# Output and down projections of a two-layer decoder trunk, with weights moved 512 wide and a residual that keeps tokens on partitions

## The chip, the cores and the metric

The kernel runs on one core of a Trainium2 chip. The metric is the device time of one execution in microseconds (us). One execution was also taken by the hardware profiler; its rows are what this document reads.

## The reference, cut to what matters

256 tokens of width 2048 go through two layers. Each layer normalises, projects to three groups of attention heads (4 differential, 6 latent, 6 forgetting), joins the 16 heads and projects back; then it normalises again and runs a gated MLP of width 5632 with a short convolution over the tokens. A last norm ends the trunk. The lines that the change touches are these:

```python
mix = jnp.concatenate([o_a, o_b, o_c], axis=-1)              # 16 heads x 128
x = x + jnp.einsum('bsm,md->bsd', mix, w_o[l])               # output projection
h = _rmsnorm(x, ffn_norm[l])
x = x + _conv_gated_mlp(h, ffn_w_up[l], ffn_conv_w[l], ffn_conv_b[l], ffn_w_down[l])
...
return _rmsnorm(x, final_norm)
```

`_conv_gated_mlp` ends with the down projection, `silu(g) * a` (256 x 5632) times `w_down` (5632 x 2048). The norm is `x * rsqrt(mean(x*x) + eps) * gain` over the 2048 features.

## The kernel before

All weights lie in memory as one stream of 128x128 blocks, in the order of use. SyncE loads 16 blocks at a time (1 MB, `load`), three such chunks in flight. `convert` splits 8 blocks at a time (a "sub") into a rounded part `hi` (ScalarE, L134) and the rest `lo` (VectorE, L135); four subs of each exist, and `weights` asks for a sub two ahead of the one in use. Activations are kept split in the same way, as one tile of 512 columns: `hi` of the 256 tokens, then `lo`. A product is hi*hi + hi*lo + lo*hi.

Two helpers build most matmuls. `mm_t` (L184 to L188) has the weight block stationary and the activations moving: per block one matmul of 512 columns (weight `hi` against both halves of the activations) and one of 256 (weight `lo` against the first half). Its result has features on partitions and tokens along the free dimension. `mm_v` (L218 to L220) turns the roles round: 128 tokens of an activation tile are stationary and 512 (or 256) columns of weights move; per step there are three matmuls for each of the two token halves, which cover four blocks. Before the change only the value projections use `mm_v`.

The residual `xT` has features on partitions: 16 tiles of 128 features x 256 tokens. The output projection runs in two passes over 16 feature tiles: pass 1 over 10 heads (L717 on), while the last six heads' attention is worked off in the background by `tick()`; pass 2 over the remaining six heads (L725 on). Each tile's result is added to `xT[m]` by two VectorE instructions (L718/719, L726/727, and L763/764 in the down projection). In pass 2 and in the second half of the down projection `norm.add` follows: ScalarE squares the tile (L350), GpSimd sums the squares (L355), ScalarE and VectorE write the next stage's split input `h` (L359, L360). `norm.cols` then sums the squares over partitions with four small matmuls (L324), and `norm.rows` spreads the factors over partitions (L339).

The MLP runs in two halves of 22 tiles; each half ends with a down projection of 16 feature tiles with 22 blocks each. After the last one every tile is scaled by the final gain (L768), the factors are spread, and VectorE multiplies eight tiles (L772), each followed by its store.

The order of instructions on each engine comes from the program order of this code, with small moves by the tile framework; a wait is a semaphore set between engines. Three PSUM banks serve the tiles called `mm`, two the tiles called `s`.

Of the kernel before, what the change touches and what calls it, by code (L numbers as in the profile page):

```python
# [58 lines left out]
def kernel(ctx: ExitStack, tc: tile.TileContext, xin, pos, wstream, cst, par, fin, out):  # L59
# [174 lines left out]
    gfin = const.tile([P, KT], F32, tag="gfin", name="gfin")  # L234
    pint = work.tile([P, T], I32, tag="tmp", name="pint", bufs=15)
    xg = [big.tile([P, 2, T], F32, tag=f"x{k}", name=f"x{k}") for k in range(KT // 2)]
# [140 lines left out]

    def score_mm(parts, bias=None):
# [100 lines left out]
    for l in range(DEPTH):  # L479
# [11 lines left out]
        else:  # L491
            first = mm_t2(hx, {KT // 2: norm.cols})
# [4 lines left out]
        if l == 0:  # L497
# [3 lines left out]
            nc.sync.dma_start(gfin, fin)  # L501
# [220 lines left out]
        norm = Norm(q_[:, Q_FN : Q_FN + KT], D)  # L722
        hx = [big.tile([P, 2 * T], F32R, tag=f"h{k}", name=nm("h")) for k in range(KT)]
        for m in range(KT):
            ps = mm_t([mix[i] for i in range(4, 10)])  # L725
            nc.vector.tensor_tensor(xT[m], xT[m], ps[:, :T], ALU.add)  # L726
            nc.vector.tensor_tensor(xT[m], xT[m], ps[:, T : 2 * T], ALU.add)  # L727
            norm.add(xT[m], m, hx[m])
        rstd = None

        for half in range(2):
            acts = []
            for i in range(HALF):
                ft = half * HALF + i
                ys = []
                for j in range(2):
                    ps = mm_t(hx, {KT // 2: norm.cols} if rstd is None else {})
                    rstd = rstd or norm.rows("rstd")
                    u = total(ps)
# [13 lines left out]
            last = half == 1  # L753
            if last:
                final = l == DEPTH - 1
                if not final:
                    norm = Norm(pr[l + 1][:, Q_AN : Q_AN + KT], D)
                    hx = [big.tile([P, 2 * T], F32R, tag=f"h{k}", name=nm("h")) for k in range(KT)]
                else:
                    norm = Norm(None, D)  # L760
            for m in range(KT):
                ps = mm_t(acts)
                nc.vector.tensor_tensor(xT[m], xT[m], ps[:, :T], ALU.add)  # L763
                nc.vector.tensor_tensor(xT[m], xT[m], ps[:, T : 2 * T], ALU.add)
                if last:
                    norm.add(xT[m], m, None if final else hx[m])
                    if final:
                        nc.scalar.activation(xT[m], xT[m], AF.Copy, scale=gfin[:, m : m + 1])  # L768

    rows = spread((norm.cols(), norm.dg)[1]).rearrange("p (j t) -> p j t", j=1).to_broadcast([P, 2, T])  # L770
    for g in range(KT // 2):
        nc.vector.tensor_tensor(xg[g], xg[g], rows, ALU.mult)  # L772
        (nc.sync, nc.scalar)[g % 2].dma_start(out[g], xg[g])


def _layout(inputs):
# [20 lines left out]
    for l in range(DEPTH):  # L797
# [25 lines left out]
        stat(np.concatenate([wo[10 * P :], wo[: 4 * P]], axis=0))  # L823
        stat(wo[4 * P : 10 * P])
        up, dn = w["ffn_w_up"][l], w["ffn_w_down"][l]
        for half in range(2):
            for i in range(half * HALF, (half + 1) * HALF):
                stat(up[:, i * P : (i + 1) * P])
                stat(up[:, FF + i * P : FF + (i + 1) * P])
            stat(dn[half * HALF * P : (half + 1) * HALF * P])  # L830
# [11 lines left out]
    for l in range(DEPTH):  # L842
# [30 lines left out]
        "x": np.ascontiguousarray(w["x"].reshape(T, KT // 2, 2, P).transpose(1, 3, 2, 0)),  # L873
        "pos": np.ascontiguousarray(np.broadcast_to(w["positions"].reshape(1, T), (P, T))),
# [3 lines left out]
        "fin": np.ascontiguousarray(w["final_norm"].reshape(KT, P).T),  # L878
# [20 lines left out]
```

## Time and profile before

| what | value |
|---|---|
| median of 3 timed runs (2298.13 to 2301.83) | 2298.94 us |
| the profiled execution, its span from first to last instruction | 2297.5 us |
| median of the runs less that span | 1.44 us |
| matmuls | 12956 |
| TensorE busy | 2270.6 us, 99% |
| VectorE busy | 1580.0 us, 69% |
| ScalarE busy | 1234.2 us, 54% |
| mean granted TensorE clock | 0.997 |

The page has no own time for the profiled execution beside its span. A busy time of TensorE counts matmuls that overlap: ends are modelled, so what a matmul costs is read from the distance between two starts, not from its length.

### The profile page before, as it was taken

The numbers are of one execution on the slowest core, as the hardware profiler recorded it, in microseconds if no ns is written. First come the engines' busy times: TensorE is split into PE (matmuls) and PEld (weight loads), VectorE is DVE, ScalarE is ACT, GpSimd is POOL, SyncE is SP. The second block draws the span as 40 slices with busy tenths as digits, with TensorE's granted clock in tenths as the row PEclk, the third lists the DMA queues.
The fourth block names the chain that finished last, engine by engine and source line by source line (L and its number), as shares of the span: only waits on it lengthen the run. The fifth ranks groups of instructions, "written<-read, shape, count | busy, mean of one in ns | idle before, by whom it ended". The sixth has DMA issues, their size and how long they took to land.

```text
span 2297.5 us, 33344 instructions
## 1 busy us (share of the span) xinstructions
PE 2270.6 (99%) x12956; PEld 1965.8 (86%) x12956; DVE 1580.0 (69%) x2512; ACT 1234.2 (54%) x1878; POOL 447.6 (19%) x445
## 2 busy tenths in 40 slices
PE   8999999999999999999999999999999999999997
PEld 7888988888888888888888889888888888888886
DVE  7768768777765577776664777687777556777654
ACT  6456645655543455554454665466555435555543
POOL 5500002222210022221140110032222001222211
PEclk9999999999999999999999999999999999999999
DMA  7544434555555555555555444345555555555553
GB/s 257 186 163 165 149 140 171 183 183 186 188 187 190 184 184 185 185 191 185 189 185 183 152 162 164 129 173 189 188 184 183 186 187 191 188 184 183 185 186 116
DMA packets 60062, 410.59 MB, mean 179 GB/s; under 512 B 6912, under 2 KB 7040, under 8 KB 11136
## 3 DMA queue, kind: packets, MB, share of 16 engines
q1 hardware_dynamic: 59184, 407.40, 49.8%
q8 instruction: 101, 1.65, 0.3%
q10 hardware_dynamic: 720, 1.07, 0.1%
q14 instruction: 57, 0.47, 0.1%
HBM read 406.35 MB, written 2.10 MB: 178 GB/s over the span
## 4 chain that ended last, share of the span: by engine, by line
PE 96%; DVE 3%; issue 1%; ACT 0%; DMA 0%; POOL 0%; DVEq 0%; ACTq 0%
PE mm L184 52%; PE mm L185 26%; PE mm L188 3%; PE mm L218 2%; PE mm L219 2%; PE mm L220 2%; PE s L386 2%; PE mm L187 2%; DVE h L360 1%; PE mm L205 1%; DVE lo L135 1%; PE mm L678 1%; PE mm L679 1%; PE mm L680 1%; PE pv L418 1%
## 5 line engine op out<-in xcount | busy, mean ns | idle before, releaser
L135 DVE TENSOR_TENSOR lo<-raw,hi 128x1024 fp32r<-128x1024 f32 (+1 forms) x775 | 988.7, 1276 | 454.3 <-ACT hi L134 449.7
L184 PE MATMUL mm<-h,hi 128*128 128x512 f32 x3435 | 1225.4, 399 | 0.6 <-DVE x L727 0.6
L134 ACT CAST hi<-raw 128x1024 fp32r<-128x1024 f32 (+1 forms) x775 | 807.4, 1042 | 596.7 <-PE mm L184 444.8
L185 PE MATMUL mm<-h,lo 128*128 128x256 f32 x3435 | 964.1, 281 | 0.0
L184 PEld LDWEIGHTS mm<-h,hi 128*128 128x128 f32 x3435 | 645.5, 188 | 151.6 <-issue 1.7
L185 PEld LDWEIGHTS mm<-h,lo 128*128 128x128 f32 x3435 | 648.5, 189 | 9.8
L184 PE MATMUL mm<-slot,hi 128*128 128x512 f32 x1792 | 640.0, 399 | 3.4 <-DVE x L727 3.4
L185 PE MATMUL mm<-slot,lo 128*128 128x256 f32 x1792 | 503.1, 281 | 0.0
L184 PEld LDWEIGHTS mm<-slot,hi 128*128 128x128 f32 x1792 | 336.7, 188 | 87.0 <-issue 5.1
L185 PEld LDWEIGHTS mm<-slot,lo 128*128 128x128 f32 x1792 | 338.4, 189 | 4.7
L741 POOL TENSOR_TENSOR tmp<-tmp,rstd 128x256 f32<-128x256 f32 x176 | 131.1, 745 | 736.3 <-DVE tmp L229 721.2
L227 ACT COPY tmp<-mm 128x256 f32<-128x256 f32 (+1 forms) x233 | 86.7, 372 | 161.1 <-PE mm L188 159.5
L749 POOL TENSOR_TENSOR tmp<-tmp,tmp 128x256 f32<-128x256 f32 x88 | 120.2, 1366 | 268.6 <-ACT tmp L748 264.9
L355 POOL TENSOR_TENSOR tmp<-tmp,tmp 128x256 f32<-128x256 f32 x64 | 78.5, 1227 | 454.1 <-ACT tmp L350 453.3
L744 ACT ACTIVATE tmp<-tmp,par 128x256 f32<-128x256 f32 x176 | 105.7, 601 | 66.5 <-POOL tmp L741 66.4
L229 DVE TENSOR_TENSOR tmp<-mm,tmp 128x256 f32<-128x256 f32 (+1 forms) x233 | 97.6, 419 | 53.2 <-ACT tmp L227 53.1
L424 DVE TENSOR_TENSOR slot<-tmp,slot 128x256 fp32r<-128x256 f32 x96 | 41.2, 429 | 92.5 <-ACT slot L423 92.5
L423 ACT CAST slot<-tmp 128x256 fp32r<-128x256 f32 x96 | 39.0, 406 | 108.0 <-POOL tmp L749 106.3
L188 PE MATMUL mm<-h,hi 128*128 128x512 f32 x229 | 91.4, 399 | 0.0
L746 DVE SCALAR_TENSOR_TENSOR tmp<-tmp,par,tmp 128x254 f32<-128x254 f32 x176 | 85.0, 483 | 6.2
L745 DVE SCALAR_TENSOR_TENSOR tmp<-tmp,par,tmp 128x255 f32<-128x255 f32 x176 | 83.3, 473 | 1.3 <-ACT tmp L744 1.3
L218 PE MATMUL mm<-hi,h 128*128 128x512 f32 (+1 forms) x192 | 68.3, 356 | 0.0
(183 smaller groups left out, 1815.0 us busy)
## 6 DMA issues: line engine op xcount, KB each, us to landing
raw<-in_w SPq DMA_DIRECT2D x381, 1024.0 KB, 4.8
raw<-in_w SPq DMA_DIRECT2D x12, 256.0 KB, 5.4
x<-in_x SPq DMA_DIRECT2D x8, 256.0 KB, 5.3
out<-x SPq DMA_DIRECT2D x4, 256.0 KB, 2.3
out<-x ACTq DMA_DIRECT2D x4, 256.0 KB, 2.4
raw<-in_w SPq DMA_DIRECT2D x1, 512.0 KB, 3.4
par<-in_par SPq DMA_DIRECT2D x1, 325.0 KB, 6.3
par<-in_par SPq DMA_DIRECT2D x1, 304.0 KB, 5.2
```

The costliest lines, as they stand in the source:

```text
L134: nc.scalar.copy(hi[:, a], src[:, a])
L135: nc.vector.tensor_tensor(lo[:, a], src[:, a], f(hi[:, a]), ALU.subtract)
L184: nc.tensor.matmul(ps, hi, mv, start=(i == 0), stop=False)
L185: nc.tensor.matmul(ps[:, :T], lo, mv[:, :T], start=False, stop=False)
L188: nc.tensor.matmul(ps, hi, mv, start=False, stop=True)
L218: nc.tensor.matmul(ps[t][:, :n], s_hi, hi, start=(i == 0), stop=False)
L227: nc.scalar.copy(t[:rows], ps[:rows, T : 2 * T])
L229: nc.vector.tensor_tensor(u[:rows], ps[:rows, :T], t[:rows], ALU.add)
L741: nc.gpsimd.tensor_tensor(uu, u, rstd, ALU.mult)
L744: nc.scalar.activation(y, uu, AF.Identity, scale=q_[:, w + 2 : w + 3], bias=q_[:, w + 3 : w + 4])
L746: nc.vector.scalar_tensor_tensor(y[:, 2:], uu[:, : T - 2], q_[:, w : w + 1], y[:, 2:], ALU.mult, ALU.add)
L749: nc.gpsimd.tensor_tensor(ys[0], ys[0], ys[1], ALU.mult)
```

## The change

The output projection and the down projection use `mm_v` with 512 columns of weights moving, so their results have tokens on partitions. The residual becomes `xr`, two tiles of 128 tokens x 2048 features; it is loaded by two transfers of 1 MB. The first layer's input still comes in with features on partitions (into slots that are free later). `residual` runs four column groups j of 512 features; after each, two VectorE adds of 512 columns follow. In a stage that feeds a norm, ScalarE squares and sums each piece (`RowNorm.add`), and eight TensorE transposes (`RowNorm.turn`) bring four feature tiles back to features on partitions, hooked in before step 2 of the next column group (the last four tiles: before step 4 of the next projection). The first pair of up-projection tiles is built by `mm_t2`, which interleaves two feature tiles. The final gain is multiplied in by GpSimd (the last group by VectorE), and the output is stored with tokens on partitions.

```diff
-    def mm_v(stat, n, every):
+    def mm_v(stat, n, every, hooks={}):
...
+            if i in hooks:
+                hooks[i]()
...
-            if i % every == every - 1:
+            if every and i % every == every - 1:
                 tick()
...
+    xr = [big.tile([P, D], F32, tag=f"x{t}", name=f"x{t}") for t in range(2)]
+    xg = [slot().rearrange("p (j t) -> p j t", j=2) for k in range(KT // 2)]
...
+    class RowNorm:
...
+        def add(self, j, t):
+            a = slice(j * 512, (j + 1) * 512)
+            nc.scalar.activation(slot(), xr[t][:, a], AF.Square, accum_out=self.sums[:, t, j : j + 1])
+
+        def turn(self, j):
+            for g in range(2):
+                ps = bank("s", 2)
+                ks = [4 * j + 2 * g + i for i in range(2)]
+                for i, k in enumerate(ks):
+                    for t in range(2):
+                        o = i * T + t * P
+                        nc.tensor.transpose(ps[:, o : o + P], xr[t][:, k * P : (k + 1) * P], ident)
+                for i, k in enumerate(ks):
+                    x, hl, gk = ps[:, i * T : (i + 1) * T], self.hl[k], self.gain[:, k : k + 1]
+                    nc.scalar.activation(hl[:, :T], x, AF.Copy, scale=gk)
+                    nc.vector.scalar_tensor_tensor(hl[:, T : 2 * T], x, gk, f(hl[:, :T]), ALU.mult, ALU.subtract)
+
+        def cols(self):
...
+                nc.vector.tensor_reduce(r, self.sums, mybir.AxisListType.X, ALU.add)
+                nc.scalar.activation(r, r, AF.Sqrt, scale=1.0 / D, bias=e_main)
+                nc.vector.reciprocal(r, r)
...
+    def residual(stat, every, after=None):
+        for j in range(4):
+            ps = mm_v(stat, 512, every, {2: (lambda: after(j - 1))} if after and j else {})
+            for t in range(2):
+                a = slice(j * 512, (j + 1) * 512)
+                nc.vector.tensor_tensor(xr[t][:, a], xr[t][:, a], ps[t], ALU.add)
+                if after:
+                    norm.add(j, t)
...
-            first = mm_t2(hx, {KT // 2: norm.cols})
+            first = mm_t2(hx, {4: lambda: norm.turn(3), KT // 2: norm.cols})
...
-            nc.sync.dma_start(gfin, fin)
+            for t in range(2):
+                nc.sync.dma_start(xr[t], xnat[t])
...
-        for m in range(KT):
-            ps = mm_t([mix[i] for i in order])
-            nc.vector.tensor_tensor(xT[m], xT[m], ps[:, :T], ALU.add)
-            nc.vector.tensor_tensor(xT[m], xT[m], ps[:, T : 2 * T], ALU.add)
-            tick()
+        residual([mix[i] for i in order], 2)
...
+        norm = RowNorm(q_[:, Q_FN : Q_FN + KT], hx)
+        residual([mix[i] for i in range(4, 10)], 0, norm.turn)
...
+                    pair = mm_t2(hx, {4: lambda: norm.turn(3), KT // 2: norm.cols})
+                    rstd = norm.rows("rstd")
...
+            if half == 0:
+                residual(acts, 0)
+            elif l < DEPTH - 1:
...
+                residual(acts, 0, norm.turn)
+            else:
+                gf = [slot() for _ in range(4)]
+                for j in range(4):
+                    nc.sync.dma_start(gf[j], fin[:, j * 512 : (j + 1) * 512])
...
+                        e = nc.vector if j == 3 else nc.gpsimd
+                        e.tensor_tensor(xr[t][:, a], xr[t][:, a], gf[j], ALU.mult)
...
+    col = norm.cols()
+    for j in range(4):
+        a = slice(j * 512, (j + 1) * 512)
+        nc.vector.tensor_scalar(xr[0][:, a], xr[0][:, a], col[:, 0:1], None, ALU.mult)
+        nc.sync.dma_start(out[0][:, a], xr[0][:, a])
+        nc.scalar.activation(xr[1][:, a], xr[1][:, a], AF.Copy, scale=col[:, 1:2])
+        nc.scalar.dma_start(out[1][:, a], xr[1][:, a])
```

The weight stream keeps its blocks and its length; within these projections they are laid down row by row of 512 columns.

The order on TensorE in the last down projection. Before, each weight block (`hi`, `lo`) is the stationary operand of two matmuls, named behind the comma, and one activation tile (`slot`) moves:

```order
L184 MATMUL mm_21719<-slot_18524,hi_21663 128x512
L185 MATMUL mm_21719<-slot_18524,lo_21664 128x256
L184 MATMUL mm_21719<-slot_18635,hi_21663 128x512
L185 MATMUL mm_21719<-slot_18635,lo_21664 128x256
L184 MATMUL mm_21719<-slot_18746,hi_21663 128x512
L185 MATMUL mm_21719<-slot_18746,lo_21664 128x256
L184 MATMUL mm_21719<-slot_18857,hi_21663 128x512
L185 MATMUL mm_21719<-slot_18857,lo_21664 128x256
```

After, the `slot` is stationary and 512 columns of `hi` or `lo` move; two accumulators (one for each half of the tokens) take turns:

```order
L220 MATMUL mm_20362<-hi_20486,slot_19540 128x512
L221 MATMUL mm_20362<-lo_20487,slot_19540 128x512
L222 MATMUL mm_20362<-hi_20486,slot_19540 128x512
L220 MATMUL mm_20363<-hi_20486,slot_19540 128x512
L221 MATMUL mm_20363<-lo_20487,slot_19540 128x512
L222 MATMUL mm_20363<-hi_20486,slot_19540 128x512
```

Four blocks stand for eight matmuls in the first piece and for six in the second.

The order on VectorE in pass 2 of layer 0. Before (L726, L727 are the adds, L360 writes the second half of `h`, L135 is the conversion of weights):

```order
L726 TENSOR_TENSOR x_78<-x_78,mm_3747 128x256
L727 TENSOR_TENSOR x_78<-x_78,mm_3747 128x256
L360 SCALAR_TENSOR_TENSOR h_3708<-x_78,par_73,h_3708 128x256
L135 TENSOR_TENSOR lo_3799<-raw_3696,hi_3798 128x1024
L360 SCALAR_TENSOR_TENSOR h_3709<-x_78,par_73,h_3709 128x256
L726 TENSOR_TENSOR x_79<-x_79,mm_3767 128x256
L135 TENSOR_TENSOR lo_3827<-raw_3772,hi_3826 128x1024
L727 TENSOR_TENSOR x_79<-x_79,mm_3767 128x256
L726 TENSOR_TENSOR x_79<-x_79,mm_3793 128x256
L727 TENSOR_TENSOR x_79<-x_79,mm_3793 128x256
L360 SCALAR_TENSOR_TENSOR h_3710<-x_79,par_73,h_3710 128x256
```

After (L426 are the adds, L401 writes `h` from the transposed tiles `s`), from the end of column group 0 to the end of column group 1:

```order
L426 TENSOR_TENSOR x_77<-x_77,mm_3615 128x512
L135 TENSOR_TENSOR lo_3682<-raw_3643,hi_3681 128x1024
L426 TENSOR_TENSOR x_78<-x_78,mm_3616 128x512
L135 TENSOR_TENSOR lo_3718<-raw_3643,hi_3717 128x1024
L401 SCALAR_TENSOR_TENSOR h_3598<-s_3693,par_73,h_3598 128x256
L401 SCALAR_TENSOR_TENSOR h_3600<-s_3702,par_73,h_3600 128x256
L401 SCALAR_TENSOR_TENSOR h_3599<-s_3693,par_73,h_3599 128x256
L401 SCALAR_TENSOR_TENSOR h_3601<-s_3702,par_73,h_3601 128x256
L135 TENSOR_TENSOR lo_3734<-raw_3685,hi_3733 128x1024
L426 TENSOR_TENSOR x_77<-x_77,mm_3673 128x512
L135 TENSOR_TENSOR lo_3760<-raw_3685,hi_3759 128x1024
L426 TENSOR_TENSOR x_78<-x_78,mm_3674 128x512
```

Eight adds of 256 columns per four feature tiles have become two of 512; the four writes of `h` stay, and now wait for TensorE's transposes.

## Rows read from the trace of the kernel before

**Rows 1.** The page: busy time and share of the span; the chain by engine.
```profile
PE 2270.6 (99%) x12956; PEld 1965.8 (86%) x12956; DVE 1580.0 (69%) x2512; ACT 1234.2 (54%) x1878; POOL 447.6 (19%) x445
...
PE 96%; DVE 3%; issue 1%; ACT 0%; DMA 0%; POOL 0%; DVEq 0%; ACTq 0%
```

**Rows 2.** Windows by stage: stretch, length, busy us by engine, granted clock, DMA.
```profile
287.90:362.80 74.90, 74.90 (x413) 61.74 (x412) 50.69 (x124) 32.74 (x57) 0.00 (x0) 1.00 0.42 150
362.80:413.30 50.50, 47.24 (x266) 40.00 (x265) 45.78 (x73) 31.35 (x53) 17.67 (x15) 1.00 0.47 167
...
650.60:775.60 125.00, 124.80 (x706) 107.91 (x705) 67.06 (x79) 47.69 (x48) 2.20 (x2) 1.00 0.52 185
...
1498.60:1548.60 50.00, 47.54 (x266) 40.08 (x265) 45.78 (x72) 31.12 (x53) 17.68 (x15) 1.00 0.47 169
...
1786.00:1910.40 124.40, 124.40 (x706) 107.87 (x705) 67.10 (x78) 47.78 (x48) 2.04 (x2) 1.00 0.52 186
...
2283.60:2297.50 13.90, 1.84 (x9) 1.45 (x8) 6.78 (x14) 2.47 (x4) 0.00 (x0) 0.60 0.40 151
```

**Rows 3.** Timeline of TensorE, first column the start: down projection, its first matmul and the next stage's.
```profile
650.63 0.40 PE L184 MATMUL mm<-slot,hi 128*128 128x512 f32 x1
...
775.59 0.40 PE L184 MATMUL mm<-h,hi 128*128 128x512 f32 x1
```

**Rows 4.** Timeline of TensorE: a value projection, 96 matmuls of 512 columns, then 256.
```profile
88.07 0.40 PE L218 MATMUL mm<-hi,h 128*128 128x512 f32 x1
...
109.84 0.28 PE L218 MATMUL mm<-hi,h 128*128 128x256 f32 x1
...
110.20 0.29 PE L218 MATMUL mm<-hi,h 128*128 128x256 f32 x1
```

**Rows 5.** Timeline of TensorE: transposes of one head and the matmuls behind them.
```profile
176.20 0.27 PE L409 MATMUL pt<-cs,tmp 128*128 128x128 f32 x1
176.31 0.27 PE L410 MATMUL pt<-cs,tmp 128*128 128x128 f32 x1
...
176.45 0.48 PE L218 MATMUL mm<-hi,h 128*128 128x512 f32 x1
176.76 0.40 PE L219 MATMUL mm<-lo,h 128*128 128x512 f32 x1
```

**Rows 6.** One line's instructions: length in ns, least, median and most.
```profile
L409 PE MATMUL pt<-cs,tmp x32: 270/272/273, 139.9 to 1469.4; 128*128 128x128 f32 x32
```

**Rows 7.** The chain that ended last, in pass 2: start, us, what.
```profile
390.51 1.43 issue
391.94 1.35 DVE h L360 x2
```

**Rows 8.** Groups by line and form: busy us, mean ns of one, idle before.
```profile
L135 DVE TENSOR_TENSOR lo<-raw,hi 128x1024 fp32r<-128x1024 f32 x763 | 980.6, 1286 | 449.2 <-ACT hi L134 444.7
...
L360 DVE SCALAR_TENSOR_TENSOR h<-x,par,h 128x256 fp32r<-128x256 f32 x64 | 45.5, 734 | 0.4 <-ACT h L359 0.2
...
L573 ACT ACTIVATE slot<-mm,rcol 128x512 f32<-128x512 f32 x12 | 7.8, 685 | 2.0 <-PE mm L220 2.0
...
L305 DVE TENSOR_TENSOR slot<-slot,sinT 128x512 f32<-128x512 f32 x8 | 5.5, 690 | 0.4
```

**Rows 9.** The chain at the end of the program.
```profile
2283.42 0.24 PE mm L188
2283.68 0.43 DVE x L763
...
2285.63 1.28 ACT L328
...
2289.08 0.69 DVE x L772
```

**Rows 10.** The page: loads of weights, count, size, us to landing.
```profile
raw<-in_w SPq DMA_DIRECT2D x381, 1024.0 KB, 4.8
```

**Rows 11.** Waits: who waited for whom, us in total, times, longest.
```profile
ACT hi L134 <- PE mm L184: 444.8, 350, 3.6
...
ACT hi L134 <- DMA raw<-in_w: 2.6, 1, 2.6
```

More of the change, by code (lines that the diff above doesn't have):

```diff
@@ L58, with kernel @@
 @with_exitstack
-def kernel(ctx: ExitStack, tc: tile.TileContext, xin, pos, wstream, cst, par, fin, out):
+def kernel(ctx: ExitStack, tc: tile.TileContext, xin, xnat, pos, wstream, cst, par, fin, out):
     nc = tc.nc
@@ L376, in rows, with __init__ @@
             return r
+    class RowNorm:
+        def __init__(self, gain, hl):
+            self.gain, self.hl = gain, hl
+            self.sums = work.tile([P, 2, 4], F32, tag="sums", name=nm("sums"), bufs=2)
+            self.col = None
+        def add(self, j, t):
[14 more added lines that the diff above has]
+        def cols(self):
+            if self.col is None:
+                r = work.tile([P, 2], F32, tag="rcol", name=nm("rcol"), bufs=6)
+                nc.vector.tensor_reduce(r, self.sums, mybir.AxisListType.X, ALU.add)
+                nc.scalar.activation(r, r, AF.Sqrt, scale=1.0 / D, bias=e_main)
+                nc.vector.reciprocal(r, r)
+                self.col = r
+            return self.col
+        def rows(self, tag):
+            r = self.cols()
+            dg = tmp()
+            for t in range(2):
+                nc.vector.tensor_scalar(dg[:, t * P : (t + 1) * P], ident, r[:, t : t + 1], None, ALU.mult)
+            rows = keep(tag)
+            nc.scalar.copy(rows, spread(dg))
+            return rows
+    def residual(stat, every, after=None):
[6 more added lines that the diff above has]
+                    norm.add(j, t)
     def score_mm(parts, bias=None):
@@ L500 @@
                 nc.sync.dma_start(pr[i], par[i])
-            nc.sync.dma_start(gfin, fin)
+            for t in range(2):
+                nc.sync.dma_start(xr[t], xnat[t])
         kr = slot()
@@ L735 @@
                 ys = []
+                if rstd is None:
+                    pair = mm_t2(hx, {4: lambda: norm.turn(3), KT // 2: norm.cols})
+                    rstd = norm.rows("rstd")
+                else:
+                    pair = None
                 for j in range(2):
-                    ps = mm_t(hx, {KT // 2: norm.cols} if rstd is None else {})
-                    rstd = rstd or norm.rows("rstd")
-                    u = total(ps)
+                    u = total(pair[j] if pair else mm_t(hx))
                     uu = tmp()
@@ L752, with gain @@
                 acts.append(a)
[L753 to L773, printed above, removed]
+            if half == 0:
+                residual(acts, 0)
+            elif l < DEPTH - 1:
+                hx = [big.tile([P, 2 * T], F32R, tag=f"h{k}", name=nm("h")) for k in range(KT)]
+                norm = RowNorm(pr[l + 1][:, Q_AN : Q_AN + KT], hx)
+                residual(acts, 0, norm.turn)
+            else:
+                gf = [slot() for _ in range(4)]
+                for j in range(4):
+                    nc.sync.dma_start(gf[j], fin[:, j * 512 : (j + 1) * 512])
+                norm = RowNorm(None, None)
+                def gain(j):
+                    a = slice(j * 512, (j + 1) * 512)
+                    for t in range(2):
+                        e = nc.vector if j == 3 else nc.gpsimd
+                        e.tensor_tensor(xr[t][:, a], xr[t][:, a], gf[j], ALU.mult)
+                residual(acts, 0, gain)
+                gain(3)
+    col = norm.cols()
+    for j in range(4):
+        a = slice(j * 512, (j + 1) * 512)
+        nc.vector.tensor_scalar(xr[0][:, a], xr[0][:, a], col[:, 0:1], None, ALU.mult)
+        nc.sync.dma_start(out[0][:, a], xr[0][:, a])
+        nc.scalar.activation(xr[1][:, a], xr[1][:, a], AF.Copy, scale=col[:, 1:2])
+        nc.scalar.dma_start(out[1][:, a], xr[1][:, a])
 def _layout(inputs):
@@ L822, in _layout @@
         wo = w["w_o"][l]
-        stat(np.concatenate([wo[10 * P :], wo[: 4 * P]], axis=0))
-        stat(wo[4 * P : 10 * P])
+        for part in (np.concatenate([wo[10 * P :], wo[: 4 * P]], axis=0), wo[4 * P : 10 * P]):
+            for j in range(4):
+                move(part[:, j * 512 : (j + 1) * 512])
         up, dn = w["ffn_w_up"][l], w["ffn_w_down"][l]
@@ L827, in _layout @@
             for i in range(half * HALF, (half + 1) * HALF):
-                stat(up[:, i * P : (i + 1) * P])
-                stat(up[:, FF + i * P : FF + (i + 1) * P])
-            stat(dn[half * HALF * P : (half + 1) * HALF * P])
+                ag = [up[:, i * P : (i + 1) * P], up[:, FF + i * P : FF + (i + 1) * P]]
+                if i == 0:
+                    move(np.concatenate(ag, axis=1))
+                else:
+                    stat(ag[0])
+                    stat(ag[1])
+            for j in range(4):
+                move(dn[half * HALF * P : (half + 1) * HALF * P, j * 512 : (j + 1) * 512])
     nblk = sum(b.shape[0] for b in blocks)
@@ L877, in _layout @@
         "par": par,
-        "fin": np.ascontiguousarray(w["final_norm"].reshape(KT, P).T),
+        "fin": np.ascontiguousarray(np.broadcast_to(w["final_norm"].reshape(1, D), (P, D))),
     }
@@ L892 @@
     ]
-    args.append(nc.dram_tensor("out_0", (KT // 2, P, 2, T), F32, kind="ExternalOutput").ap())
+    args.append(nc.dram_tensor("out_0", (2, P, D), F32, kind="ExternalOutput").ap())
     with tile.TileContext(nc) as tc:
@@ L897 @@
     y = r.results[0]["out_0"]
-    return np.ascontiguousarray(y.transpose(3, 0, 2, 1).reshape(1, T, D))
+    return np.ascontiguousarray(y.reshape(1, T, D))
```

9 lines of the change are left out of this document (1 added, 8 removed).

## The prediction

> **What bounds the kernel now.** I read the page first. TensorE is busy 99% and carries 96% of the chain [rows 1], so time changes only where TensorE's stream gets shorter or waits less. Then the windows by stage, cut where the helper lines change on TensorE: in the down projections TensorE is busy for the whole stretch and VectorE for about half of it, so these stages are paced by TensorE alone [rows 2]. Two stretches differ: pass 2 of the output projection with the first pair of up tiles (362.8 to 413.3, and the same in layer 1) has TensorE idle for some 3 of 50 us while VectorE is busy 45.8, and the last 13.9 us are a tail with almost no TensorE work [rows 2]. In pass 2 the chain leaves TensorE: it runs over VectorE's writes of `h` and waits between them [rows 7].
>
> Since lengths of matmuls overlap, I then took prices from starts. In the first down projection 352 pairs of `mm_t` fill 650.63 to 775.59, so a pair costs 0.355 us for one block [rows 3]. The value projection already runs the form that the change wants: 96 matmuls of 512 columns from 88.07 to 109.84, 0.2268 each [rows 4]. Six of them cover four blocks: 1.361 us against 4 x 0.355 = 1.420. Both forms move 3072 columns for these four blocks; what differs is that six stationary operands are loaded in place of eight.
>
> **Down projections.** Each half becomes 4 x 22 x 6 = 528 matmuls, 119.75 us at 0.2268. Two halves take 125.0 now and two 124.4, one row of each stands in [rows 2]: gain 2 x 5.25 + 2 x 4.65 = 19.8 us. The conversions of weights (one per eight blocks, VectorE 1.29 us [rows 8]) stay hidden: eight blocks last 2.72 us. The adds become two of 0.69 (taken from a 512-wide VectorE row [rows 8]) per column group, less than before.
>
> **Output projection, pass 1.** Of 74.9 us [rows 2], 160 pairs are 56.8; the rest, 18.1, is the background heads, which are the same. New: 240 x 0.2268 = 54.4. Gain 2.4 per layer, 4.8 us in all. The heads are now resumed every two steps, 2.72 us plus the head's own matmuls apart.
>
> **Pass 2 and the first up pair.** Now 50.5 and 50.0 us [rows 2], of which 128 pairs are 45.4; the other 5 are waits and the norm's small matmuls. New: 144 x 0.2268 = 32.7, the 32 up pairs 11.4, and 32 transposes. The trace has the same transposes in the heads: start to start 0.11, and the matmul behind the third one starts its successor after 0.31 in place of 0.23, so that one also costs 0.11 [rows 5]: 3.5 us. The four small matmuls that spread the factors stay, about 0.4 (estimate, four times 0.11); the four that summed squares go. Sum 48.0: gain 2.5 and 2.0, together 4.5. This needs VectorE to keep up. Before, four feature tiles give it 3 conversions, 8 adds of 0.43 and 4 writes of `h` of 0.73, 10.2 us against 24 pairs, 8.5 us of TensorE [rows 8, 9]; that is the wait in [rows 7]. After, a column group gives it 3 x 1.29 + 2 x 0.69 + 4 x 0.73 = 8.2 against 8.2 + 0.9 of TensorE. TensorE leads again, with a tenth to spare. What is late next is `h` of the last four tiles: transposed before step 4 of the first up pair, needed at its step 12, eight steps or 5.7 us later; four writes of 0.73 fit.
>
> **Layer 1's attention norm** gets the same 32 transposes, 3.5 us, and loses four small matmuls, 0.4: loss 3.1 us.
>
> The price of a transpose is the weakest one. From above it is its length, 0.272 [rows 6]; from below nothing at all, if it hid under its neighbours. Three sets of 32: 0 to 26.1 us, and I take 10.6, as the row nearest to it (same shape, same type, in a row) says.
>
> The clock stays out of it: the stretch with six heads' transposes has a granted clock of 1.00, the upper level of 2.4 GHz (its first row) [rows 2]. The Trainium skill (TensorE: Matmul & The Clock Gate, Part 4: PE-mode transpose) gives some 275 ns for a 128x128 transpose inside a kernel. By that figure 96 of them would be 26 us (estimate), and the time 2286; the trace agrees with it as the length of one, not as the distance of two.
>
> **Bank hand-over.** Each column group needs two of three `mm` banks, so the second accumulator of the next group waits for the first add. After a value projection's first part ScalarE frees that bank with 0.685 us of work [rows 8], and the next part's fourth matmul, which needs it, comes 0.36 us in with no gap [rows 4]. In the new code the fourth matmul comes 0.68 us in, and the add takes 0.69: more room. I price it at nothing; the cover is VectorE being free when the first accumulator ends, four matmul starts before the group's end.
>
> **Loads.** 2 MB for `xr` stand in SyncE's queue before a weight chunk in the first 30 us, and 1 MB of gains before the last projection. A 1 MB load lands in 4.8 us [rows 10]; ScalarE's conversions wait for TensorE to free buffers 445 us in all and for a load once, 2.6 us, at the start [rows 11]. So I price them at nothing; uncovered they cost up to 9.6 us.
>
> **Tail.** Now 13.9 us [rows 2]: last matmul to the first output multiply 5.4 [rows 9], then eight multiplies of 0.69 and stores. New: the second add 0.69, ScalarE's square of that piece 0.69, a table load of 1.28 and about 0.7 for root and reciprocal: 3.4, a gain of 2.0. Then ScalarE does four multiplies of about 0.69, 2.8 in place of 5.5, but issues its own stores between them; I count 1.0 of 2.7. Together 3.0; bounds 0 and 4.7.
>
> **Sum.** 19.8 + 4.8 + 4.5 - 3.1 + 3.0 = 29.0. Span 2297.5 - 29.0 = 2268.5; the timed median lies 1.44 over the span, so 2269.9, say 2270 us.
>
> **Rivals.**
> A, the sum above: 2270, own range 2262 to 2278. Chance 0.76.
> B, transposes do not overlap and cost their length: 96 x 0.162 more, 15.6 us: 2286. For it: only groups of three are seen, now eight with 512-column matmuls on both sides. Against: [rows 5]. Chance 0.07.
> C, pass 2 stays bound by VectorE. Its tenth to spare is gone if the writes of `h` wait for ScalarE, which waits for the transposes: the 5 us of waits per layer stay, 10 us: 2280. Against: fewer instructions, no GpSimd beside it. Chance 0.08.
> E, the stream does not get shorter since columns alone pace it: 19.8 + 4.8 + 1.4 x 2 lost, 2270 + 27 = 2297, no change. The value projection would then be fast for a reason of its own, and the new stages would step at 0.355 x 4 / 6 = 0.237 us. Against: [rows 3] and [rows 4] are the same core at the same granted clock. Chance 0.05. The Trainium skill states such a rule (same page, Back-to-back issue gap): an isolated matmul follows the last by its columns over 2.4 GHz plus 2.5 ns. By it four pairs are 1300 ns and six matmuls 1295, and the whole stream would gain 2.4 us (estimate). The trace is longer than the rule in both forms, by 30 ns a pair and 11 ns a matmul.
> D, slower: the bank hand-over fails. There are 32 column groups. The first add ends 0.2 us into the next group (four starts of 0.2268 before the end, 0.40 of matmul length [rows 4], 0.69 of add) and is wanted at 0.68. One conversion of 1.29 in front of it makes TensorE wait 0.8, 26 us in all: 2296. Two make it 2.1, 67 us: 2337. It decides from 0.9 us per group on (29.0 / 32). For it: VectorE works in strict order and conversions stand right beside the adds. Against: conversions run two subs ahead, and VectorE is half idle in the down projections [rows 2]. Chance 0.04.
>
> **How the numbers follow.** Two timings of this kernel can be told apart from about 0.2%, 4.6 us. A, B and C are faster: 0.91. E is no change: 0.05. D is slower: 0.04. The range takes A with its own bounds and C, and part of B: 2260 to 2284. Its low end is the sum with transposes half hidden (-5) and the tail at its best (-2), and some left over for stages I called equal.
>
> **What the profile after would show.** In the down projections: 528 matmuls of 512 columns per half, 0.227 from start to start, stretches of 119.8. Transposes 0.11 apart in groups of eight. In pass 2 no chain over VectorE; TensorE idle under 1 us. At each column group's fourth matmul no gap (D shows one of 0.8 or more). A tail near 11 us. I am wrong if the 512-column starts in the down projections lie 0.236 apart (E), if transposes lie 0.27 apart (B), or if TensorE waits for an add (D).

## The result, and the profile after

The changed kernel takes 2269.87 us (median of 4 runs, 2269.70 to 2270.36); the kernel before, beside it, 2298.53 (2296.55 to 2301.83). The ratio is 0.9874, with a 95% interval of 0.9860 to 0.9888: 28.7 us less, where 2270 was forecast. The total is right partly because two misses cancel, as the stages show.

The page after, busy time and the chain that ended last (compare [rows 1]):

```profile
PE 2248.8 (99%) x12072; PEld 1923.5 (85%) x12072; DVE 1506.2 (66%) x2316; ACT 1229.3 (54%) x1866; POOL 385.1 (17%) x395
...
PE 98%; DVE 1%; ACT 0%; DMA 0%; issue 0%; POOL 0%; ACTq 0%; SPq 0%; DVEq 0%
```

TensorE's share of the chain rose from 96% to 98%: the waits of pass 2 are gone from it. Windows of the kernel after, with the columns of [rows 2]: the start, pass 1 of both layers, pass 2 with the first up pair of both layers, the four down projections' kinds, the tail.

```profile
0.00:83.80 83.80, 77.12 (x428) 67.31 (x429) 72.48 (x124) 53.45 (x84) 51.36 (x45) 1.00 0.72 266
283.80:357.20 73.40, 73.40 (x332) 57.62 (x331) 44.42 (x100) 32.72 (x57) 0.00 (x0) 1.00 0.42 153
357.20:405.10 47.90, 47.90 (x246) 40.53 (x244) 33.32 (x47) 30.87 (x51) 0.00 (x0) 1.00 0.49 172
642.40:762.10 119.70, 119.70 (x530) 99.11 (x529) 59.50 (x55) 47.91 (x48) 2.21 (x2) 1.00 0.54 193
1010.80:1133.20 122.40, 122.40 (x554) 101.59 (x553) 64.89 (x67) 57.11 (x72) 2.22 (x2) 1.00 0.52 189
1482.50:1530.60 48.10, 48.10 (x245) 40.47 (x244) 32.92 (x47) 29.98 (x52) 0.00 (x0) 1.00 0.48 175
1768.10:1887.80 119.70, 119.70 (x530) 99.15 (x529) 59.69 (x55) 48.01 (x48) 2.08 (x2) 1.00 0.54 193
2256.40:2268.60 12.20, 0.00 (x0) 0.00 (x0) 3.95 (x9) 5.65 (x10) 0.00 (x0) 0.60 0.46 172
...
1408.30:1482.50 74.20, 73.59 (x333) 57.65 (x332) 43.41 (x100) 32.25 (x57) 0.00 (x0) 1.00 0.39 142
```

Three windows of the kernel before that [rows 2] does not hold: the start, pass 1 of layer 1, and the second down projection of layer 0.

```profile
0.00:88.10 88.10, 79.35 (x429) 68.78 (x430) 75.14 (x124) 53.19 (x84) 61.61 (x52) 0.98 0.64 230
...
1423.70:1498.60 74.90, 74.90 (x413) 61.75 (x412) 49.91 (x123) 32.48 (x57) 0.00 (x0) 1.00 0.39 141
...
1024.30:1149.30 125.00, 124.79 (x706) 107.91 (x705) 79.39 (x93) 58.42 (x78) 21.73 (x16) 1.00 0.53 185
```

Put side by side, stage by stage (us, after less before, from the starts on TensorE in the two profiled executions):

| stage | forecast | measured |
|---|---|---|
| start, to the first value projection | 0 | -4.2 |
| output projection, pass 1, two layers | -4.8 | -2.1 |
| pass 2 with the first up pair, two layers | -4.5 | -4.6 |
| four down projections and layer 1's attention with its norm | -16.7 | -16.4 |
| tail | -3.0 | -1.6 |
| the rest | 0 | 0.1 |
| sum | -29.0 | -28.8 |

The forecast for the fourth row is 19.8 less the 3.1 that layer 1's norm was to lose. The up projections did not move: 237.33 and 248.74 us.

Of the marks that the forecast set, the tail near 11 us is not there (12.2 in the window above); the others are. The first down projection, 528 matmuls in 119.7 us, goes at 0.2267. Timeline of TensorE after, eight transposes in one row and the matmuls behind them (start, length, engine, line, what):

```profile
1043.48 1.03 PE L397 MATMUL s<-cs,x 128*128 128x128 f32 x8
1044.27 0.48 PE L220 MATMUL mm<-hi,slot 128*128 128x512 f32 x1
1044.58 0.40 PE L221 MATMUL mm<-lo,slot 128*128 128x512 f32 x1
```

From 1043.48 to 1044.27 the eight take 0.79, and the matmul behind them hands over (from its start to the next start) after 0.31 in place of 0.23: 0.87 in all, 0.109 each. And the end of a column group, TensorE with VectorE:

```profile
671.85 0.69 DVE L426 TENSOR_TENSOR x<-x,mm 128x512 f32<-128x512 f32 x1 [1.09 <-PE mm L222]
...
672.33 0.39 PE L220 MATMUL mm<-hi,slot 128*128 128x512 f32 x1
...
673.00 0.39 PE L220 MATMUL mm<-hi,slot 128*128 128x512 f32 x1
```

The next group starts at 672.33, the first add is over at 672.54 (0.21 into it, as forecast), and the fourth matmul, at 673.00, needs the bank and finds it free.

### The profile page after: what moved, and what is told of

Same layout as the page of the kernel before. It is cut to its first block, busy times and chain, and to the rows that moved or that the text cites. A ratio compares the mean times of both kernels' runs of the same rounds, so it can differ in the third digit from the quotient of the medians.

```text
span 2268.6 us, 31133 instructions
## 1 busy us (share of the span) xinstructions
PE 2248.8 (99%) x12072; PEld 1923.5 (85%) x12072; DVE 1506.2 (66%) x2316; ACT 1229.3 (54%) x1866; POOL 385.1 (17%) x395
## 4 chain that ended last, share of the span: by engine, by line
PE 98%; DVE 1%; ACT 0%; DMA 0%; issue 0%; POOL 0%; ACTq 0%; SPq 0%; DVEq 0%
PE mm L184 35%; PE mm L185 18%; PE mm L220 12%; PE mm L222 11%; PE mm L221 11%; PE mm L188 2%; PE s L438 2%; PE mm L205 1%; PE mm L187 1%; PE mm L203 1%; PE pv L470 1%; PE s L397 0%; PE mm L731 0%; PE mm L732 0%; PE mm L733 0%; PE pv L471 0%
## 5 line engine op out<-in xcount | busy, mean ns | idle before, releaser
L135 DVE TENSOR_TENSOR lo<-raw,hi 128x1024 fp32r<-128x1024 f32 (+1 forms) x775 | 988.5, 1276 | 520.6 <-ACT hi L134 516.2
L184 PE MATMUL mm<-h,hi 128*128 128x512 f32 x3375 | 1203.9, 399 | 0.0
L134 ACT CAST hi<-raw 128x1024 fp32r<-128x1024 f32 (+1 forms) x775 | 808.2, 1044 | 588.6 <-PE mm L222 379.4
L185 PE MATMUL mm<-h,lo 128*128 128x256 f32 x3375 | 947.1, 281 | 0.0
L184 PEld LDWEIGHTS mm<-h,hi 128*128 128x128 f32 x3375 | 634.1, 188 | 148.5 <-issue 1.7
L185 PEld LDWEIGHTS mm<-h,lo 128*128 128x128 f32 x3375 | 637.1, 189 | 9.5
L220 PE MATMUL mm<-hi,slot 128*128 128x512 f32 x992 | 388.1, 391 | 0.6 <-DVE slot L735 0.6
L221 PE MATMUL mm<-lo,slot 128*128 128x512 f32 x992 | 384.8, 388 | 0.0
L222 PE MATMUL mm<-hi,slot 128*128 128x512 f32 x992 | 384.7, 388 | 0.0
L220 PEld LDWEIGHTS mm<-hi,slot 128*128 128x128 f32 x992 | 186.3, 188 | 42.5 <-issue 4.0
L222 PEld LDWEIGHTS mm<-hi,slot 128*128 128x128 f32 x992 | 186.3, 188 | 38.3
L221 PEld LDWEIGHTS mm<-lo,slot 128*128 128x128 f32 x992 | 186.4, 188 | 36.9
L797 POOL TENSOR_TENSOR tmp<-tmp,tmp 128x256 f32<-128x256 f32 x88 | 119.9, 1362 | 262.1 <-ACT tmp L796 262.1
L188 PE MATMUL mm<-h,hi 128*128 128x512 f32 x225 | 89.8, 399 | 0.0
## 6 DMA issues: line engine op xcount, KB each, us to landing
x<-in_xn SPq DMA_DIRECT2D x2, 1024.0 KB, 10.8
```

The lines of the kernel that those rows point to most:

```text
L134: nc.scalar.copy(hi[:, a], src[:, a])
L135: nc.vector.tensor_tensor(lo[:, a], src[:, a], f(hi[:, a]), ALU.subtract)
L184: nc.tensor.matmul(ps, hi, mv, start=(i == 0), stop=False)
L185: nc.tensor.matmul(ps[:, :T], lo, mv[:, :T], start=False, stop=False)
L188: nc.tensor.matmul(ps, hi, mv, start=False, stop=True)
L797: nc.gpsimd.tensor_tensor(ys[0], ys[0], ys[1], ALU.mult)
```

## The experiments

**Half of the down projections.** The kernel before, with the 512-wide form in the first half of each layer's MLP only:

```diff
+            if not last:
+                for j in range(4):
+                    ps = mm_v(acts, 512, 99)
+                    for t in range(2):
+                        xw = xg[2 * j + t][:].rearrange("p j t -> p (j t)")
+                        nc.vector.tensor_tensor(xw, xw, ps[t], ALU.add)
+                continue
```

> The kernel before, in which only the first half's down projection of each layer uses the form with 512 columns of weights moving (two adds of 512 columns per group into the old residual; the stream is unchanged, so these two projections add the wrong products, and the output is not the reference's). Theory, the pace comes from the number of matmuls and stationary loads: 528 matmuls of 0.2268 us in place of 352 pairs of 0.355, 119.7 in place of 125.0 us twice, so about 10.5 us less than before: 2288. Rival, columns alone pace it: 0 less, 2298.5.

Measured: 2288.56 against 2297.48, ratio 0.9961 (0.9946 to 0.9977), 8.9 us less. Its windows of a changed and of an unchanged down projection:

```profile
649.95:769.63 119.68, 119.68 (x529) 99.13 (x528) 59.49 (x55) 47.99 (x48) 2.21 (x2) 1.00 0.54 193
1018.37:1143.35 124.98, 124.76 (x706) 107.90 (x705) 79.40 (x93) 58.50 (x78) 21.70 (x16) 1.00 0.52 185
```

The 5.3 us belong to the new form and order of the matmuls; no transpose and no new residual is in this kernel. The theory's 10.5 counted 125.0 us for both stages; layer 1's goes from 124.4 [rows 2] to 119.7, so the traces give 10.0, and the timed 8.9 agrees with that within its interval (5 to 12 us). The rival that columns alone pace TensorE falls. What in the new form wins the time, this run does not tell; the last experiment takes it apart.

**Every transpose twice.** The changed kernel:

```diff
-                        nc.tensor.transpose(ps[:, o : o + P], xr[t][:, k * P : (k + 1) * P], ident)
+                        for _ in range(2):
+                            nc.tensor.transpose(ps[:, o : o + P], xr[t][:, k * P : (k + 1) * P], ident)
```

> The changed kernel with each of the 96 transposes issued twice in a row (same result written again). Theory, a transpose costs the distance of two starts, 0.109 us, all of it on the path: 96 x 0.109 = 10.5 more, 2280.4. Rival, it costs its length of 0.272: 26 more, 2296. Rival, it hides under its neighbours: 0 more, 2270.

Measured: 2280.55 (2280.28 to 2280.69), 10.7 us above the changed kernel: 96 more transposes at 0.11. The price per transpose stands, with nothing of it hidden and nothing of it at its length of 0.27.

**The two adds in the other order.** The changed kernel, with the loop over the two accumulators turned round:

```diff
-            for t in range(2):
+            for t in (1, 0):
```

> The changed kernel with the two adds of each column group in the other order, so that the accumulator that TensorE wants back first is added last. Theory, the bank hand-over is free only because the first add ends in time: the first accumulator's add now ends some 1.55 us into the next group and is wanted at 0.68, so TensorE waits about 0.87 us at each of 31 hand-overs, 27 more: 2297. Rival, the hand-over has slack in any order (a bank is not reused so soon): 0 more, 2270.

Measured: 2270.33. The theory's 27 us did not come, but the run says nothing about them: what ran was not what was written. VectorE's order in the built program still has the first accumulator's add ahead in all 32 groups (`x_77`, then `x_78`), and TensorE's order is the same, row for row:

```
L426 TENSOR_TENSOR x_77<-x_77,mm_3056 128x512
L426 TENSOR_TENSOR x_78<-x_78,mm_3057 128x512
```

The framework had put the add that can start first in front again.

**The bank's readers late.** The changed kernel, with more work on the first accumulator that can't be put aside:

```diff
+                if t == 0:
+                    nc.vector.tensor_tensor(xr[t][:, a], xr[t][:, a], ps[t], ALU.add)
+                    nc.vector.tensor_tensor(xr[t][:, a], xr[t][:, a], ps[t], ALU.subtract)
```

> The changed kernel, with the first accumulator of each column group read by VectorE twice more (added, taken away, added again). In VectorE's order the bank's last reader then comes behind the other accumulator's add and, in 29 of 32 groups, a conversion of weights: 3 x 0.69 + 0.69 + 1.25 from 0.48 us before the next group, so its end is 3.5 us into that group where the fourth matmul wants the bank at 0.68. Theory (the bank hand-over decides once it is late, as in the prediction's slower rival): TensorE waits some 2.8 us in 31 groups, 87 us in all: 2357, between 2335 and 2365. Rival: the third bank and the conversions ahead cover most of it: 2270 to 2290.

Measured: 2272.50 (2272.20 to 2272.88), not 2357. VectorE, behind a column group that ends at 702.34:

```profile
701.86 0.69 DVE L427 TENSOR_TENSOR x<-x,mm 128x512 f32<-128x512 f32 x1 [1.09 <-PE mm L222]
702.47 1.22 DVE L135 TENSOR_TENSOR lo<-raw,hi 128x1024 fp32r<-128x1024 f32 x1
703.60 0.68 DVE L428 TENSOR_TENSOR x<-x,mm 128x512 f32<-128x512 f32 x1
704.20 1.28 DVE L429 TENSOR_TENSOR x<-x,mm 128x512 f32<-128x512 f32 x2
```

The last reader ends at 705.48, 3.1 us into the next group, late as intended. But TensorE's matmuls go on at 0.227, twelve of them in 2.72 us:

```profile
702.34 0.39 PE L220 MATMUL mm<-hi,slot 128*128 128x512 f32 x1
...
705.06 0.39 PE L220 MATMUL mm<-hi,slot 128*128 128x512 f32 x1
```

The order of the program shows why: the changed kernel gives each accumulator three matmuls in turn; here a group of a down projection, unless it is the stage's first, begins with 12 on its first accumulator (the free third bank), and then come 12 on the second. Nor does that second accumulator take the late bank: the built program gives it the bank of the other add, the first of the two on L429, which ends at 704.88, ahead of the thirteenth matmul at 705.06. The late bank is used again only a group later. So the framework placed TensorE's matmuls and the banks around the delay. My expectation took both as given; they aren't. The run does not bring out the slower rival's price, since TensorE never asked for the late bank. The profiled execution is 2.3 us longer than the changed kernel's; 0.7 of it lie ahead of the last matmul's start, the rest in the tail, which waits for the two adds more.

**Two banks in place of three.** The changed kernel:

```diff
-        ps = [bank("mm", 3) for _ in range(2)]
+        ps = [bank("mm", 2) for _ in range(2)]
```

(and the same for the other tiles called `mm`)

> The changed kernel with two PSUM banks in place of three for all tiles called mm. Each column group then needs the bank of the group before for its first matmul, not for its fourth. Theory (the bank hand-over costs what the first add is late, and the framework's order lets the first accumulator run ahead of the second, as it did in the run with late readers): the first add ends 0.2 us into the next group, so TensorE waits 0.2 to 0.3 in each of 32 groups, 6 to 10 us, and a little in the value projections, which free a bank in the same way: 2276 to 2282. Rival without that reordering: each group also waits for the second add, which ends 1.9 us in where the fourth matmul wants it at 0.7: 32 x 1.4 = 45 us, 2315. Rival that banks are not what matters here: 2270.

Measured: 2310.95, ratio to the kernel before 1.0053 (1.0036 to 1.0070). Most of the 41 us come from the start and the attention, whose causes this run does not separate: its first value projection begins 16 us later than the changed kernel's, and the attention takes 4.5 us more in layer 0 and 8 in layer 1. In the residual's column groups the theory holds, as a group's end shows:

```profile
726.23 0.39 PE L222 MATMUL mm<-hi,slot 128*128 128x512 f32 x1
726.72 0.50 PE L220 MATMUL mm<-hi,slot 128*128 128x512 f32 x1
727.06 0.39 PE L221 MATMUL mm<-lo,slot 128*128 128x512 f32 x1
```

TensorE waits 0.26 for the add, and the first matmul behind the wait costs 0.1 more; the first down projection takes 121.45 in place of 119.69. In the built order the first accumulator again runs six to eight matmuls ahead of the second. Some 0.4 us a group is what a missing bank costs there; in layer 1's first down projection (122.2 us in place of 119.7) it is 0.6.

**The start.** The kernel before, with the first norm's epsilon made to depend on a later conversion of weights, so that ScalarE's wait for the norm comes behind it:

```diff
-                self.col, self.dg = inv_rms(self.acc, self.n, e_main)
+                self.col, self.dg = inv_rms(self.acc, self.n, getattr(self, "eps", e_main))
...
+            late = small(1)
+            nc.vector.tensor_scalar(late, f(subs[7][1][:, :1]), 0.0, EPS, ALU.mult, ALU.add)
+            norm.eps = late
```

> The kernel before, with one change at the start: the square root of the first norm reads its epsilon from a value that depends on the sixth and seventh conversion (same number), so that ScalarE does these conversions before it waits for the norm's sums. Theory, the first 88 us were 4.2 us longer before the change only because ScalarE's queue stood at that square root while TensorE ran out of converted weights, and TensorE's clock fell behind the pause: 4 less, 2294.5. Rival, the start's 4 us come from the new kernel's other loads or from chance: no change, 2298.5.

Measured: 2295.38 against 2297.48, ratio 0.9992 (0.9984 to 1.0001): in the theory's direction, half its size, and the interval reaches no change. The trace shows the effect itself. ScalarE before: the square root (L328) waits 4.12 us for TensorE's column sums, and conversions of weights (L134) are queued behind it:

```profile
22.38 1.28 ACT L328 ACT_TABLE_LOAD   x1
27.77 0.26 ACT L328 ACTIVATE rcol<-misc,cs 128x2 f32<-128x2 f32 x1 [4.12 <-PE misc L324]
27.93 1.98 ACT L134 CAST hi<-raw 128x1024 fp32r<-128x1024 f32 x2
```

ScalarE in the changed kernel: two conversions stand in front of the norm.

```profile
22.25 2.00 ACT L134 CAST hi<-raw 128x1024 fp32r<-128x1024 f32 x2
...
27.25 0.26 ACT L330 ACTIVATE rcol<-misc,cs 128x2 f32<-128x2 f32 x1 [1.70 <-PE misc L326]
```

Windows of 25 to 35 us, before:

```profile
25.00:30.00 5.00, 3.63 (x25) 3.05 (x23) 1.59 (x4) 2.23 (x4) 4.85 (x6) 1.00 0.57 221
30.00:35.00 5.00, 4.67 (x19) 4.06 (x19) 4.97 (x8) 2.75 (x5) 4.93 (x2) 0.66 0.46 157
```

In the changed kernel:

```profile
25.00:30.00 5.00, 5.00 (x34) 4.48 (x33) 4.92 (x8) 2.96 (x5) 4.93 (x3) 1.00 1.01 411
30.00:35.00 5.00, 5.00 (x32) 4.44 (x32) 3.35 (x4) 3.13 (x5) 4.78 (x4) 1.00 1.01 418
```

In the run with the epsilon, the second window:

```profile
30.00:35.00 5.00, 4.59 (x29) 3.90 (x28) 4.62 (x8) 3.56 (x6) 4.78 (x4) 1.00 0.84 306
```

Before, TensorE stands idle for 1.4 us, and in the window behind it the mean granted clock is 0.66, so part of that window runs at the lower of the two levels (1.2 GHz, the upper is 2.4): 19 matmuls in five microseconds where 32 fit. In the run with the epsilon both windows have a clock of 1.00, and its first value projection begins at 83.95, as after (83.84), not at 88.07 [rows 4]. So the order does it in the traces, where it is worth 4.1 us; what it is worth in a timed run lies between nothing and 3.7.

**Whole blocks stored.** The changed kernel, with the output laid out in blocks:

```diff
-        nc.sync.dma_start(out[0][:, a], xr[0][:, a])
+        nc.sync.dma_start(out[0][j], xr[0][:, a])
...
```

> The changed kernel, with each piece of the output (128 tokens x 512 features) stored as one whole block of 256 KB in place of 128 rows of 2 KB with gaps between them (the output's pieces are put together differently, the values are the same). Theory: the tail is set by 2.1 MB that leave at some 380 GB/s whatever their shape, 5.5 us: 2270, within 0.3. Rival: the rows cost something each, and whole blocks shorten the stores by a quarter or more: 2268.5 or less.

Measured: 2270.17, as the theory has it. The shape of the stores is not what sets the tail.

**Lengths grouped by two and by four.** The changed kernel, `mm_t` taking its blocks in groups (2, and in another run 4), the 512-column matmuls of a group first and then the 256-column ones:

```diff
...
+        for at in range(0, k, GRP):
...
+            last = at + GRP >= k
+            for wide_ in ((False, True) if last else (True, False)):
+                for i, mv, hi, lo in grp:
+                    if wide_:
+                        nc.tensor.matmul(ps, hi, mv, start=(i == 0), stop=(i == k - 1))
+                    else:
+                        nc.tensor.matmul(ps[:, :T], lo, mv[:, :T], start=False, stop=False)
```

> In the changed kernel, the projections that keep features on partitions issue two 512-column matmuls and then two 256-column ones, in place of one and one in turn; nothing else changes. Theory: the turn from one length to the other costs time. Pairs step at 0.3534 us in the up projections; 512-column matmuls in a row at 0.2268 and 256-column ones in a row at 0.1199, together 0.3467. With half the turns, the some 2750 pairs of the up projections win half of 0.0067 each, 9 us: about 2261. If the turn costs nothing until two are side by side, up to 18: 2252. Rival: what makes 0.3534 is the load of weights (0.15 us busy for each on average), which does not fit beside a matmul of 0.12; two short matmuls side by side then make it worse: 2275 to 2300. Second rival: the order within a pair has no influence: 2270.

> As the run with pairs by two, with four 512-column matmuls and then four 256-column ones. Theory of the turns: a quarter of the turns is left, gain 14 us, about 2256. Rival on the load of weights: as slow as by two or slower. Rival of no influence: 2270.

Measured: by two 2257.60 (2257.12 to 2257.98), ratio to the kernel before 0.9823 (0.9807 to 0.9840); by four 2260.22 (2259.43 to 2260.50). The second up stage of layer 0, after:

```profile
762.09:1010.83 248.74, 248.74 (x1410) 215.71 (x1409) 177.92 (x241) 145.24 (x216) 62.46 (x64) 1.00 0.52 186
```

By two:

```profile
758.13:1004.22 246.09, 246.09 (x1410) 214.99 (x1409) 171.70 (x241) 143.44 (x216) 60.55 (x64) 1.00 0.53 188
```

704 pairs go from 248.74 to 246.09, from 0.3533 to 0.3496 each; with the first stage (237.33 to 234.96) that is 5.0 us a layer, near the theory's first figure (9 us for both layers). So taking the two lengths in turn costs time. By four the second stage takes 246.40: nothing more is won, the theory's figure for it (14 us) fails, and with it the idea that every turn costs the same. What sets the rest, 0.003 a pair over the 0.3467 of two long streams, isn't settled, nor why a turn costs. By two is the version that beats both kernels, by 40.5 and by 12.3 us.

**The kernel before, grouped by two.** The same edit of `mm_t`, in the kernel before:

> The kernel before, with two 512-column matmuls and then two 256-column ones in all projections that keep features on partitions, the output and down projections among them. Theory (part of what the change wins in those projections is the turn from one length to the other, which costs about 0.0035 us a pair): 10 us in the up projections and 2 in the attention's as in the changed kernel, 1408 pairs of the down projections 5, 512 of the output projections 1.5 or nothing where VectorE paces them: 2279 to 2281. Between this and the changed kernel with the same grouping then lie 22, not 28.7 us. Rival (the gain of the down projections has nothing to do with turns, only with six stationary operands in place of eight): only 12 us as in the changed kernel, 2286.

Measured: 2280.75 (2278.89 to 2280.86), ratio 0.9921 (0.9907 to 0.9936), 17.1 us less, as the theory has it. Its first down projections of layer 0 and of layer 1:

```profile
646.71:769.90 123.19, 122.89 (x706) 107.14 (x704) 67.19 (x79) 47.78 (x48) 2.14 (x2) 1.00 0.53 188
...
1774.07:1896.54 122.47, 122.47 (x705) 107.05 (x704) 67.27 (x78) 47.90 (x48) 1.91 (x2) 1.00 0.53 189
```

So what a down projection gains can be taken apart, in layer 1 first. There 124.4 becomes 122.5 with half the turns; the other half, if 352 pairs go at 0.3467, is 0.4; and 176 matmuls fewer at 0.013 are 2.3 (twice a 256-column matmul, 0.120 by [rows 4], less one of 512, 0.2268, is what a matmul costs beside its columns). Sum 4.6, measured 4.7. In layer 0 a down projection gains 5.3, and the 0.6 on top is neither turns nor matmuls but a wait. In the kernel before, the first feature tile wants the last of the 22 activation tiles 7 us into the stage, and ScalarE and VectorE are still writing it (loads of weights, `PEld`, with their waits):

```profile
657.88 0.41 ACT L423 CAST slot<-tmp 128x256 fp32r<-128x256 f32 x1 [1.57 <-POOL tmp L749]
...
658.32 0.42 DVE L424 TENSOR_TENSOR slot<-tmp,slot 128x256 fp32r<-128x256 f32 x1 [1.07 <-ACT slot L423]
658.34 0.19 PEld L187 LDWEIGHTS mm<-slot,lo 128*128 128x128 f32 x1 [0.46 <-ACT slot L423]
...
658.80 0.19 PEld L188 LDWEIGHTS mm<-slot,hi 128*128 128x128 f32 x1 [0.27 <-DVE slot L424]
```

The same happens at 1032.04, in layer 0's second down projection. In the new form the first column group comes to that activation tile 28.6 us into the stage (126 matmuls at 0.2267), and the wait is gone. With the same grouping the change is worth 23.2 us, not 28.7.

## Why the prediction was right, and where it was not

**Down projections: right in price, part right in cause.** 0.2267 a matmul and 119.7 a stage were read from the value projection and came out so. But the text put the whole difference down to six stationary operands in place of eight. In layer 1 the fewer matmuls are 2.3 of the 4.7, and the rest, 1.9 of it measured, are the turns between two lengths, which the new form does not have. In layer 0 another 0.6 is the wait for the last activation tile. The forecast had it in its 125.0 without seeing it, and so also in its price of 0.355 a pair; without it a pair costs 0.353 (124.4 for 352).

**Transposes: right.** 96 at 0.11, by the row that was nearest in kind [rows 5]; shown by doubling them. Rival B, the length as the price, would have been 15.6 us higher. The Trainium skill's figure for a transpose (TensorE: Matmul & The Clock Gate, Part 4: PE-mode transpose), some 275 ns, is once more the length of one; no run here pays it as a distance.

**Pass 2: right, to a tenth of a microsecond** (47.9 and 48.1 against 48.0), and rival C falls: TensorE is busy for the whole window, VectorE 33 of 48 us where it was 45.8.

**Bank hand-over: right in result.** Its slack was as worked out. The slower rival's price (0.8 to 2.1 us a group) was paid by no column group in any run: it took TensorE's order as fixed, and the framework reorders it. With a bank less a group lost 0.4 to 0.6. The one place where the fear came true was not listed: at the entry to pass 1 in layer 1 the second accumulator takes a bank that the projection before still holds.

```profile
1408.89 0.39 PE L222 MATMUL mm<-hi,slot 128*128 128x512 f32 x1
1409.89 0.50 PE L220 MATMUL mm<-hi,slot 128*128 128x512 f32 x1 [0.61 <-DVE slot L735]
```

From start to start that is 1.00 in place of 0.23, 0.8 us lost once.

**Pass 1: mis-sized, 2.1 for 4.8.** The background heads between the projection's chunks cost the same (17.5 us before and after), but the projection's own matmuls did not cost what a stream of them does. Added up from start to start in layer 0 they take 57.3 before and 55.9 after (56.8 and 54.4 in the prediction). Nine times the first matmul behind a head hands over late:

```profile
288.72 0.50 PE L220 MATMUL mm<-hi,slot 128*128 128x512 f32 x1
289.05 0.39 PE L221 MATMUL mm<-lo,slot 128*128 128x512 f32 x1
289.29 0.40 PE L222 MATMUL mm<-hi,slot 128*128 128x512 f32 x1
```

0.33 in place of 0.23, 0.9 us in all. The next ten or so still step at up to 0.24, some 0.4 more, and the entry, where the second accumulator comes late, costs 0.2. Before, the same 0.1 was paid nine times too, but there it was hidden in a price that was too high: 0.355 a pair, from the first down projection with its wait, where the pairs of pass 1 less those nine ran at 0.353. The stream after had no such margin. In layer 1 the bank above takes 0.8 more.

**Start: not in the sum, 4.2 in the traces.** The text put a price on the loads there and none on the order. The order of ScalarE's first 50 instructions, to be had before the run, shows two conversions move ahead of the square root; with the 4.12 of wait beside it, that was a term to write down. It made good what pass 1 and the tail fell short.

**Tail: 1.6 for 3.0.** The first store is issued 3.9 us after the last matmul ends (at 2260.26, the matmul at 2256.35), before it was 6.2 (2289.79 and 2283.64): 2.2 earlier. The stores then land 3.8 us after issue in place of 2.3, and from the first issue to the end it is 8.3 us in place of 7.7, so that 1.6 is left. SyncE's stores and a window among the stores, before:

```profile
2289.79 3.95 SPq L773 DMA_DIRECT2D out<-x  x4
...
2293.00:2294.00 1.00, 0.00 (x0) 0.00 (x0) 0.95 (x2) 0.00 (x0) 0.00 (x0) 0.50 1.04 389
```

And after:

```profile
2260.26 2.42 SPq L826 DMA_DIRECT2D out<-x  x4
...
2264.00:2265.00 1.00, 0.00 (x0) 0.00 (x0) 0.00 (x0) 0.00 (x0) 0.00 (x0) 0.50 1.04 391
```

The 16 DMA engines are full in both, and 2.1 MB take 5.5 us at that rate. The 1.0 us counted for fewer multiplies could not come: they were never what the stores waited for, once the first was out. The Trainium skill (DMA: Bandwidth & Descriptors, Specifications) gives a limit of about 358 GB/s between HBM and a core; this trace is above it, with 391 in the stores here and 418 in the loads at the start.

**Loads: wrong and harmless.** A row of the page after has the two of 1 MB for the residual:

```profile
x<-in_xn SPq DMA_DIRECT2D x2, 1024.0 KB, 10.8
```

10.8 us, not 4.8: they share the engines with weights in a stretch at 411 to 418 GB/s. None of TensorE's waits in that trace is for a conversion behind them.

## What to carry to other kernels

Price a new form of work by a stretch of the same trace that already runs it, start to start; check that the old form's stretch has no wait in it, since a wait would pass for its price; and then look for what the new stretch has besides: breaks, the first matmul behind a wait, the hand-over from the stage before. Read the built order of every engine at the start and at each stage's edge, not only where the edit is: a framework moves work on its own, to your gain, to your loss, or so that an experiment tests nothing, as two did here. Where matmuls of two lengths alternate, try them two by two.

## What was not expected of the hardware

A 512-column and a 256-column matmul in turn cost 0.3533 us, although streams of each cost 0.2268 and 0.120; two and two they cost 0.3496 a pair (0.3479 in layer 1's first down projection). A matmul costs about 0.013 us beside its columns. The Trainium skill (TensorE: Matmul & The Clock Gate, Back-to-back issue gap) says that loads of weights and matmuls together set the pace in a kernel, with 131 ns for 512 columns; no stretch here comes below 0.2267, so for these fp32 streams its figure does not hold. A first matmul behind transposes or a head costs 0.1 us more than the next.
